# A decoder block's last stages: output tiles of the last two units from another pool and their LayerNorms in another order, m of y_a's second half in z's tiles, and later splits of y_a's weights, y_a's first input and T1

## The chip, the cores and the metric

The kernel runs on one NeuronCore of a Trainium2 chip. Its engines are TensorE (PE in the profile), VectorE (DVE), ScalarE (ACT), GpSimd (POOL) and SyncE (SP), which here only issues DMAs. Each engine works through its own instructions in the order in which they were issued; semaphores tie the engines together. The metric is the time of one execution in microseconds of device time, the median of several runs.

## The reference

The block takes x (2048 positions by 1024 channels, float32) and computes, cut to what matters:

```python
proj = x @ w_in + b_in                      # q, k, v, g_attn, u_lru, g_lru, gate_logits
attn = combine(dilated_attention(q, k, v))  # three head groups, weighted by softmax of their lse
y_a = (attn * silu(g_attn)) @ w_attn_proj
h = rg_lru(causal_conv(u_lru))
y_b = (h * silu(g_lru)) @ w_lru_proj
merged = sigmoid(gA) * y_a + sigmoid(gB) * y_b
out = merged @ w_out + b_out
x = layer_norm(alpha * x + out) * ln_gain + ln_bias
```

## The kernel before, in words

Each float32 product is made of three matmuls of a fast format: an operand is split into a high part h (ScalarE copies it) and a low part l (VectorE subtracts h), and h·h, h·l and l·h are added in PSUM. Such a split is one `split` of lines 1134 (ScalarE) and 1135 (VectorE), and it waits for the load of its operand. The engines' order is the order of the code (a manual schedule). Two lists move work: `later(lag, fn)` runs fn in the `run(late)` that comes lag steps on, `pe_later` does so in the middle of a step's matmuls.

Five stages follow each other on TensorE. The projection (line 636) takes 1400 us, attention 220. Then:

- **y_b**, 32 steps `yb_job(n)` of 24 matmuls, four chunks c of 512 positions by eight feature tiles f. A step first runs what is due (splits, stores), has SP load gB of step n + 2, makes its matmuls, and VectorE evacuates the tile into gB (line 1372, the evacuation), which SP stores a step later. Beside it branch A is combined: `combine` loads three head groups' outputs, `mix` has TensorE spread the weights into a bank bc (line 1315, three banks), VectorE multiplies (1316), GpSimd adds (1318, 1319), and SP stores to at_scr. In steps 23 to 31 y_a's weights wa, its input at (four parts for the first chunk) and w_out's blocks woB are loaded and, some steps later, split.
- **y_a**, 32 steps `ya_job(i)` of twelve matmuls, 2.72 us each. A tile needs its weight wa and all four input parts of its chunk; the low part of an input is read by the second of each three matmuls. VectorE forms gA = (gA + 1)·y_a (line 1481), GpSimd adds y_b (1482). The sum m stays in SBUF for chunks 0 and 1 (tiles me); for chunks 2 and 3, i = 16 to 31, it is made in place in gA's tile and stored to m_scr (1484). gA and ybr are loaded three steps ahead; gA's tiles come from five buffers of tag gt, ybr's from four of tag rc.
- **z**, the output projection in Strassen-like form: 256 positions are a unit pair q (0 to 7) with seven products each, in the table `order`; T1 to T4 are differences of w_out's blocks, loaded in y_a's last steps and behind them. `prep_m` splits the m operand two products ahead (tiles mh and ml, three buffers each), ScalarE seeds banks with the bias (line 1593), `z_outs` on VectorE forms the results, among them bank Z from bank A (line 1609), into which the third and fourth products go.
- **LayerNorm** of unit (q, i), i = 0 or 1, follows in steps behind its products: sum and mean, square, factor, norm, gain (VectorE, into an output tile), bias (GpSimd, 229), store (SP, 1680). Output tiles have tag rc, four buffers. The last pair q = 7 has a form of its own: `bn_stats` and an aggregate on VectorE (1699, 1703), the factor on GpSimd, `last_centre` (1709), and then for i = 0 a scale on ScalarE (1767) and the bias on GpSimd, for i = 1 both in one on VectorE (1714).

NZ is the number of products in `order`; the last product is NZ - 1.

Of the kernel before, what the change touches and what calls it, by code (L numbers as in the profile page):

```python
# [15 lines left out]
P = 128  # L16
# [15 lines left out]
def hybrid_block_kernel(ctx: ExitStack, tc: tile.TileContext, a: dict, out: bass.AP):  # L32
# [63 lines left out]
    def later(lag, fn):  # L96
        late.append((now["n"] + lag, fn))
# [1226 lines left out]
    def prep_wa(f, lag):  # L1324
        if f % 4 == 0:
            WA["t"] = big(("X3", "X4")[f // 4], [P, 4, 2, 4, P], F32R, f"wa{f}")
        t = WA[f] = WA["t"][:, f % 4]
        sp.dma_start(flat(t[:, 1]), wf_scr[f][:, 0:4])
        later(lag, lambda: split(t[:, 0], t[:, 1]))
# [86 lines left out]
    for n in range(32):  # L1416
        if n >= 1:
            next(blocks_of_out, None)
        c, f = divmod(n, 8)
        if c + 1 < NCH:  # L1420
            for k in range(2 * f, 2 * f + 2) if f < 4 else ():
                load_h(c + 1, k, min(k + 2, 7) - f)
        elif f < 4:
            for k in range(2 * f, 2 * f + 2):
                prep_wa(k, k + 2 - f if k < 6 else 4)
        for _ in range(2 if n in (23, 24, 28, 29, 30, 31) else 0):
            load_wo(*wo_raw.pop(0))
        if n == 26:
            for k in range(4):
                load_at(0, k, k + 2)  # L1430
        for k in range(1 if 26 <= n < 30 else 2 if n >= 30 else 0):
            later(0, lambda q=wo.pop(0): split_wo(*q))
        yb_job(n)
        if n >= 30:
            load_ya(n - 30)
        if n in cmb:
            combine(*cmb[n])
            if cmb[n][1] == 0:
                pe_later(1, lambda c=cmb[n][0]: spread(c))
        if n == 0:  # L1440
            load_stats()
        if n == 1:
            weigh()
    load_ya(2)
    for _ in range(5):
        run(late)
        run(pe_late)
        now["n"] += 1
# [16 lines left out]
    def ya_job(i):  # L1465
        c, f = divmod(i, 8)
        if i + 3 < 32:
            load_ya(i + 3)
        ga, yb = YG.pop(i)
        if i == 4:  # L1470
            ya = fp.tile([P, 4, P], F32, tag="ct", name=f"ya{c}{f}", bufs=1).rearrange("p b q -> p (b q)")
        else:
            ya = fp.tile([P, CH], F32, tag="y", name=f"ya{c}{f}", bufs=4)
        for k in range(4):
            xx = AT[c][:, k]
            pe.matmul(ya, WA[f][:, 0, k], xx[:, 0], start=(k == 0), stop=False)
            pe.matmul(ya, WA[f][:, 0, k], xx[:, 1], start=False, stop=False)
            pe.matmul(ya, WA[f][:, 1, k], xx[:, 0], start=False, stop=(k == 3))
        if f == 0 and c < 2:
            ME[c] = big(("Z0", "Z1")[c], [P, 8, CH], F32, f"me{c}")  # L1480
        dve.scalar_tensor_tensor(out=ga, in0=ga, scalar=1.0, in1=ya, op0=ALU.add, op1=ALU.mult)
        pool.tensor_tensor(out=ME[c][:, f] if c < 2 else ga, in0=ga, in1=yb, op=ALU.add)
        if c > 1:
            later(1, lambda: sp.dma_start(m_scr[c][:, f], ga))

    def load_x(q, i):
        tt_ = 2 * q + i
# [50 lines left out]
    for i in range(32):  # L1538
        run(late)
        c, f = divmod(i, 8)  # L1540
        if f == 0 and c + 1 < NCH:
            for k in range(4):
                load_at(c + 1, k, k + 4)
        if i in (2, 4, 6):
            load_vec(i // 2 - 1)
        if i == 10:
            dve.tensor_tensor(out=vec[0][:, CH:], in0=vec[0][:, CH:], in1=vec[0][:, 0:CH], op=ALU.subtract)
        if i in (8, 10, 12, 14):
            load_x(i // 4 - 2, i // 2 % 2)
        ya_job(i)  # L1550
        if wo:
            split_wo(*wo.pop(0))
        if 24 <= i < 28:
            load_tb("T1", i - 24)
        if i >= 28:
            load_tb("T2", i - 28)
            split_tb("T1", i - 28)
            if i < 30:
                prep_m(order[i - 28][0], UNIT[order[i - 28][1]])
        now["n"] += 1  # L1560
# [101 lines left out]
            act.activation(of(q, n), of(q, n), AF.Identity, scale=s[:, 10:11], bias=s[:, 11:12])  # L1662

    def out_tile(q, i, j):
        y = stats[q, i, j] = rc_p.tile([P, CH], F32, tag="rc", name=f"y{q}{i}{j}")
        return y

    def ln_gain(q, i):
# [38 lines left out]
    def last_centre(q, i, j):  # L1707
        mv = small(q, i)
        dve.scalar_tensor_tensor(out=out_tile(q, i, j), in0=of(q, LN[i][j]), scalar=mv[:, 0:1], in1=vec[1][:, SIDE[j]],
                                 op0=ALU.subtract, op1=ALU.mult)  # L1710

    def last_scale(q, i, j):
        y = stats[q, i, j]
        dve.scalar_tensor_tensor(out=y, in0=y, scalar=small(q, i)[:, 2:3], in1=vec[2][:, SIDE[j]], op0=ALU.mult, op1=ALU.add)

    whole, half_a, half_b = slice(0, CH), slice(0, CH // 2), slice(CH // 2, CH)
    for q in range(NQZ):
        for i in range(2):
            if q == NQZ - 1:
                continue  # L1720
            ready = [max(place[q, 6], place[q, 3]), place[q, 2]] if i == 0 else [place[q, 7], place[q, 4]]
            for j, (n, r) in enumerate(zip(LN[i][::-1], ready)):
                on(r + 1, "sum", ln_sum, q, i, j, n)
            g = max(ready) + 1
            for k, fn, d in (("mean", ln_mean, 1), ("square", ln_square, 2), ("factor", ln_factor, 3), ("norm", ln_norm, 4),
                             ("gain", ln_gain, 5), ("bias", ln_bias, 6), ("store", ln_store, 7)):
                d -= q + i == 0 and d > 1
                on(g + d, k, fn, q, i)
        for p, n in ((5, "C"), (1, "A")):
            if place[q, p] > 2:  # L1730
                on(*((place[2, 5] - 1, "seed late") if q == 2 else (max(place[q, p] - 3, 0), "seed")), seed, q, n)
        if q >= 2:
            on(place[q - 2, 6] + 1, "load", load_x, q, 0)
            on(place[q - 2, 7] + 1, "load", load_x, q, 1)
        for n, p in (("S1", 5), ("S2", 6), ("S3", 7), ("S4", 3)):
            on(max(place[q, p] - 4, 0), "add", add_m, q, n)
    for c in (2, 3):
        on(max(place[2 * c - 3, p] for p in (2, 3, 4)) - 1, "load", load_me, c)
    for n, g in (("T2", (0, 1, 2, 3)), ("T3", (3, 4, 5, 6)), ("T4", (7, 8, 9, 10))):
        for k in range(4):  # L1740
            on(g[k], "split", split_tb, n, k)
    for q in range(2):
        seed(q, "A")
# [9 lines left out]
        do(g, "store")  # L1753
    q = NQZ - 1
    z_product(NZ - 1)
    do(NZ - 1, "factor", "bias", "gain", "norm", "store")
    bn(q, 0, "C", whole, 1)
    last_mean(q, 0, 2)
    bn(q, 1, "Z1", half_a, 1)
    for j in range(2):  # L1760
        last_centre(q, 0, j)
    bn(q, 1, "Z1", half_b, 2)
    last_mean(q, 1, 3)
    do(NZ, "norm", "bias", "gain", "store")
    for j in range(2):
        last_centre(q, 1, j)
        act.activation(stats[q, 0, j], stats[q, 0, j], AF.Copy, scale=small(q, 0)[:, 2:3])
    ln_bias(q, 0)
    do(NZ + 1, "gain", "bias", "store")
    do(NZ + 2, "bias", "store")  # L1770
    do(NZ + 3, "store")
    for j in range(2):
        last_scale(q, 1, j)
        send(q, 0, j, sp)
# [61 lines left out]
```

## Time and profile before

| | us |
|---|---|
| three runs | 2083.02, 2086.12, 2087.07 |
| median | 2086.12 |
| the profiled execution | 2080.2 |
| its span | 2078.4 |
| TensorE busy | 2045.3 |
| VectorE busy | 1649.2 |
| ScalarE busy | 1185.8 |
| GpSimd busy | 589.3 |

The profile is of one execution. In its timeline a row has a start and a duration in us, the engine, the line of the code, the operation, out<-in, shapes and a count of merged instructions; in brackets stands how long the engine was idle before it and what released it. A letter q behind an engine's name is its queue (SPq issues DMAs). A row of the waits reads: who, waited for whom, us in total, times, longest. A row of windows gives busy time and counts of PE, PEld, DVE, ACT and POOL in a stretch, then the granted clock of TensorE as a share, and the DMA's share and rate. A row "x12" of the chain of waits merges twelve instructions. The kernel's stages lie at about 1624 to 1816 us (y_b), 1816 to 1903 (y_a), 1907 to 2063 (z) and 2063 to 2078 (the end).

### The profile page before, as it was taken

The numbers are of one execution on the slowest core, as the hardware profiler recorded it, in microseconds if no ns is written. First come the engines' busy times: TensorE is split into PE (matmuls) and PEld (weight loads), VectorE is DVE, ScalarE is ACT, GpSimd is POOL, SyncE is SP. The second block draws the span as 40 slices with busy tenths as digits, with TensorE's granted clock in tenths as the row PEclk, the third lists the DMA queues.
The fourth block names the chain that finished last, engine by engine and source line by source line (L and its number), as shares of the span: only waits on it lengthen the run. The fifth ranks groups of instructions, "written<-read, shape, count | busy, mean of one in ns | idle before, by whom it ended". The sixth has DMA issues, their size and how long they took to land.

```text
span 2078.4 us, 35466 instructions
## 1 busy us (share of the span) xinstructions
PE 2045.3 (98%) x11588; PEld 1686.9 (81%) x11588; DVE 1649.2 (79%) x3080; ACT 1185.8 (57%) x2482; POOL 589.3 (28%) x597
## 2 busy tenths in 40 slices
PE   8999999999999999999999999999999999999997
PEld 7888888888888888888887888888888888787885
DVE  8888789788889778778878888877999655545776
ACT  6447356446356565667666657567999411212674
POOL 1111111111111013222222232221425234355686
PEclk9999999999999999999999999999999999999998
DMA  8987989988988977778788879789896899998441
GB/s 271 275 250 247 267 271 249 284 249 271 252 280 245 324 242 196 224 212 247 231 259 264 282 223 260 246 230 357 331 340 197 256 321 314 320 375 269 142 153 71
DMA packets 379736, 535.16 MB, mean 257 GB/s; under 512 B 174816, under 2 KB 179936, under 8 KB 376032
## 3 DMA queue, kind: packets, MB, share of 16 engines
q1 hardware_dynamic: 363552, 507.12, 75.8%
q0 software_dynamic: 12256, 19.42, 5.6%
q10 hardware_dynamic: 3744, 6.36, 0.9%
q8 instruction: 92, 1.51, 0.3%
q14 instruction: 92, 0.75, 0.1%
HBM read 323.43 MB, written 193.59 MB: 249 GB/s over the span
## 4 chain that ended last, share of the span: by engine, by line
PE 75%; DMA 12%; ACT 5%; DVE 4%; SPq 2%; issue 1%; POOL 0%; DVEq 0%; POOLq 0%; ACTq 0%
PE q L636 57%; ACT p L1055 4%; PE A L1601 3%; PE o L1096 2%; PE C L1601 2%; PE Z L1601 2%; PE s L1040 2%; PE yb L1366 1%; PE yb L1367 1%; DMA at_scr<-oc 1%; PE yb L1368 1%; PE pt L1066 1%; PE g L497 1%; DMA m_scr<-gA 1%; SPq L309 1%
## 5 line engine op out<-in xcount | busy, mean ns | idle before, releaser
L636 PE MATMUL q<-xT,hS 128*128 128x512 f32 x1680 | 519.3, 390 | 0.0
L636 PE MATMUL q<-xT,l 128*128 128x512 f32 x1120 | 436.1, 389 | 0.0
L636 PE MATMUL q<-xB,hA 128*128 128x512 f32 x1248 | 388.2, 392 | 5.6 <-ACT xB L217 5.6
L636 PEld LDWEIGHTS q<-xT,hS 128*128 128x128 f32 x1680 | 314.4, 188 | 69.6 <-issue 5.2
L636 PE MATMUL q<-xB,l 128*128 128x512 f32 x904 | 353.0, 390 | 0.0
L636 PEld LDWEIGHTS q<-xB,hA 128*128 128x128 f32 x1248 | 235.0, 189 | 57.6 <-ACT xB L217 5.6
L636 PEld LDWEIGHTS q<-xT,l 128*128 128x128 f32 x1120 | 210.3, 188 | 43.8
L636 PEld LDWEIGHTS q<-xB,l 128*128 128x128 f32 x904 | 170.5, 189 | 35.6
L247 POOL DMA_DIRECT2D wS<-in_w_in_dram x70 | 61.8, 964 | 478.3 <-DMA wS<-in_w_in_dram 145.1
L1055 ACT ACTIVATE p<-p,sta 128x256 f32<-128x256 f32 (+1 forms) x384 | 172.9, 473 | 1.1 <-DVE sta L1047 1.1
L636 PE MATMUL q<-xT,hA 128*128 128x512 f32 x560 | 173.1, 391 | 0.0
L636 PE MATMUL q<-xB,hS 128*128 128x512 f32 x560 | 173.0, 390 | 0.0
L271 ACT ACTIVATE hA<-wA 128x512 fp32r<-128x512 f32 x218 | 134.0, 623 | 48.1 <-DMA wA<-in_w_in_dram 11.8
L271 ACT ACTIVATE hS<-S 128x512 fp32r<-128x512 f32 x175 | 107.9, 623 | 84.2 <-DVE S L229 17.9
L229 POOL TENSOR_TENSOR S<-S,wA 128x512 f32<-128x512 f32 x35 | 49.8, 1424 | 356.2 <-DVE S L229 210.2
L636 PEld LDWEIGHTS q<-xT,hA 128*128 128x128 f32 x560 | 104.8, 188 | 23.3 <-issue 1.8
L636 PEld LDWEIGHTS q<-xB,hS 128*128 128x128 f32 x560 | 104.8, 188 | 23.0 <-issue 1.5
L1047 DVE CUSTOM_DVE_ANT_0 p<-s,mask 128x256 f32<-128x256 f32 (+1 forms) x384 | 118.0, 376 | 0.2 <-PE s L1040 0.2
L1366 PE MATMUL yb<-h,wl 128*128 128x512 f32 x256 | 100.4, 392 | 0.0
L1367 PE MATMUL yb<-h,wl 128*128 128x512 f32 x256 | 99.9, 390 | 0.0
L1368 PE MATMUL yb<-h,wl 128*128 128x512 f32 x256 | 99.8, 390 | 0.0
L229 DVE TENSOR_TENSOR l<-wA,hA 128x512 fp32r<-128x512 f32 x113 | 78.0, 693 | 27.2 <-ACT hA L271 24.6
(455 smaller groups left out, 4289.3 us busy)
## 6 DMA issues: line engine op xcount, KB each, us to landing
wA<-in_w_in_dram SPq DMA_DIRECT2D x253, 256.0 KB, 4.6
wl_scr<-l SPq DMA_DIRECT2D x105, 512.0 KB, 4.9
l<-wl_scr SPq DMA_DIRECT2D x105, 512.0 KB, 4.5
sw<-y SPq DMA_DIRECT2D x384, 64.0 KB, 3.2
wS<-in_w_in_dram SPq DMA_DIRECT2D x70, 256.0 KB, 4.5
wS<-in_w_in_dram POOLq DMA_DIRECT2D x70, 256.0 KB, 6.6
v_scr<-vs SPq DMA_DIRECT2D x192, 64.0 KB, 3.7
B<-k_scr SPq DMA_DIRECT2D x24, 512.0 KB, 7.0
```

Of the source, the lines that this page charges most:

```text
L229: eng.tensor_tensor(out=out, in0=in0, in1=in1, op=op)
L247: pool.dma_start(t, w_part(s, x), accum_op=ALU.add)
L271: act.activation(h, r, AF.Copy)
L636: pe.matmul(bank, w[:, ks], x[:, kk, xx], start=(first and i == 0 and not onto), stop=(last and i == 11), skip_group_check=onto)
L1040: pe.matmul(s[h][:, j, lo:256], A[hs, x, n * P:(n + 1) * P], k, start=(x + y == 0), stop=(y == 1 or g == 2))
L1047: dve.tensor_tensor_reduce(out=st["p", i, j][:, h, lo:256], in0=st["s", i, j // 2][h][:, j % 2, lo:256], in1=mask[:, lo:256], scale=1.0, s ...
L1055: act.activation(p, p, AF.Exp, scale=-1.0, bias=s[:, h:h + 1], accum_out=s[:, 2 + h:3 + h])
L1096: pe.matmul(o[hs, j, :], V[:, n if x else prev(g, n), v0:v0 + 64], ptb[:, j % 2, x, h, :], start=(x == first(i, j) // P), stop=(x == 1))
L1366: pe.matmul(yb, WL[f][:, 0, k], xx[:, 0], start=(k == 0), stop=False)
L1367: pe.matmul(yb, WL[f][:, 0, k], xx[:, 1], start=False, stop=False)
L1368: pe.matmul(yb, WL[f][:, 1, k], xx[:, 0], start=False, stop=(k == 7))
L1601: pe.matmul(b[:, cs], x[:, k], w[:, k, y, cs], start=False, stop=(k == 3 and n == 2), skip_group_check=True)
```

## The change

- **Output tiles.** The four output tiles of q = 7 get tag gt (five buffers), the rest keep rc.
- **LayerNorm of unit (6, 1)**: square and factor stand one product earlier, norm, gain, bias and store two. In the code after the last product the order is written anew: (7, 0) is centred, scaled on ScalarE and biased on GpSimd before the second unit's statistics, half by half between its steps.
- **m of y_a's second half**: for i = 16 to 27 m goes to a tile of tag mh or ml (z's, three buffers each) instead of gA's tile, and is stored from there.
- **Splits**: of the weights wa 2 to 4 steps later (lag k + 4 - f), of at's first chunk two steps later (k + 4); the loop behind y_b's steps has one round more. T1's four splits stood in y_a's steps 28 to 31; now two stand in steps 30 and 31, and two behind z's products 0 and 1, T2 to T4 moving back by one to three products. No load is issued elsewhere.

The diff, cut to its core:

```diff
-                prep_wa(k, k + 2 - f if k < 6 else 4)
+                prep_wa(k, k + 4 - f)
...
-                load_at(0, k, k + 2)
+                load_at(0, k, k + 4)
...
-    for _ in range(5):
+    for _ in range(6):
         run(late)
...
-        pool.tensor_tensor(out=ME[c][:, f] if c < 2 else ga, in0=ga, in1=yb, op=ALU.add)
+        m = ME[c][:, f] if c < 2 else ga if i >= 28 else vx_p.tile([P, CH], F32, tag=("mh", "ml")[i % 2], name=f"m{i}", bufs=3)
+        pool.tensor_tensor(out=m, in0=ga, in1=yb, op=ALU.add)
         if c > 1:
-            later(1, lambda: sp.dma_start(m_scr[c][:, f], ga))
+            later(1, lambda: sp.dma_start(m_scr[c][:, f], m))
...
-            split_tb("T1", i - 28)
+            if i >= 30:
+                split_tb("T1", i - 30)
...
-        y = stats[q, i, j] = rc_p.tile([P, CH], F32, tag="rc", name=f"y{q}{i}{j}")
+        y = stats[q, i, j] = rc_p.tile([P, CH], F32, tag="rc" if q < NQZ - 1 else "gt", name=f"y{q}{i}{j}", bufs=4 if q < NQZ - 1 else 5)
...
+    def last_bias(j):
+        y = stats[NQZ - 1, 0, j]
+        tt(pool, y, y, vec[2][:, SIDE[j]], ALU.add)
...
-                d -= q + i == 0 and d > 1
+                d -= (q + i == 0 and d > 1) + (q == NQZ - 2 and i == 1) * ((d > 1) + (d > 3))
...
-    for n, g in (("T2", (0, 1, 2, 3)), ("T3", (3, 4, 5, 6)), ("T4", (7, 8, 9, 10))):
+    for n, g in (("T1", (0, 0, 0, 1)), ("T2", (2, 3, 4, 5)), ("T3", (5, 6, 7, 8)), ("T4", (8, 9, 10, 10))):
...
     z_product(NZ - 1)
-    do(NZ - 1, "factor", "bias", "gain", "norm", "store")
+    do(NZ - 1, "bias", "gain", "store")
     bn(q, 0, "C", whole, 1)
     last_mean(q, 0, 2)
-    bn(q, 1, "Z1", half_a, 1)
+    do(NZ, "bias", "store")
     for j in range(2):
         last_centre(q, 0, j)
+        act.activation(stats[q, 0, j], stats[q, 0, j], AF.Copy, scale=small(q, 0)[:, 2:3])
+    last_bias(0)
+    bn(q, 1, "Z1", half_a, 1)
     bn(q, 1, "Z1", half_b, 2)
     last_mean(q, 1, 3)
-    do(NZ, "norm", "bias", "gain", "store")
+    last_bias(1)
     for j in range(2):
         last_centre(q, 1, j)
-        act.activation(stats[q, 0, j], stats[q, 0, j], AF.Copy, scale=small(q, 0)[:, 2:3])
-    ln_bias(q, 0)
-    do(NZ + 1, "gain", "bias", "store")
-    do(NZ + 2, "bias", "store")
-    do(NZ + 3, "store")
```

VectorE at the end of y_b, before the change, from behind the evacuation of step 29 (gB tiles 20277 and 20327 are those of steps 30 and 31, at the input's parts, wa weights):

```order
L1135 TENSOR_TENSOR wa_20172<-wa_20172 128x512
L1135 TENSOR_TENSOR at_20175<-at_20175 128x512
L1135 TENSOR_TENSOR woB_20267<-woB_20267 128x512 x2
L1372 SCALAR_TENSOR_TENSOR gB_20277<-gB_20277,yb_20380 128x512
L1135 TENSOR_TENSOR wa_20172<-wa_20172 128x512
L1135 TENSOR_TENSOR at_20175<-at_20175 128x512
L1135 TENSOR_TENSOR wa_20172<-wa_20172 128x512 x2
L1135 TENSOR_TENSOR woB_20267<-woB_20267 128x512 x2
L1372 SCALAR_TENSOR_TENSOR gB_20327<-gB_20327,yb_20425 128x512
```

The two at rows are the third and fourth part of the input; the first two stand earlier, before the evacuations of steps 28 and 29. The same place with the change (gB tiles 20271 and 20319 are those of steps 30 and 31):

```order
L1135 TENSOR_TENSOR wa_20082<-wa_20082 128x512
L1135 TENSOR_TENSOR at_20175<-at_20175 128x512
L1135 TENSOR_TENSOR woB_20263<-woB_20263 128x512 x2
L1372 SCALAR_TENSOR_TENSOR gB_20271<-gB_20271,yb_20372 128x512
L1135 TENSOR_TENSOR wa_20082<-wa_20082 128x512
L1135 TENSOR_TENSOR at_20175<-at_20175 128x512
L1135 TENSOR_TENSOR woB_20263<-woB_20263 128x512 x2
L1372 SCALAR_TENSOR_TENSOR gB_20319<-gB_20319,yb_20413 128x512
L1135 TENSOR_TENSOR wa_20172<-wa_20172 128x512
L1135 TENSOR_TENSOR at_20175<-at_20175 128x512
L1135 TENSOR_TENSOR wa_20172<-wa_20172 128x512
L1135 TENSOR_TENSOR at_20175<-at_20175 128x512
```

Now all four input parts are split behind evacuation 29: the first before that of step 30, the second before that of step 31, the third and fourth behind it.

ScalarE between y_a and z, before (toT_21014 is T1, A the banks that the first two products add to, L1593 their seeds):

```order
L1134 ACTIVATE toT_21014<-toT_21014 128x512
L1523 ACTIVATE mh0A_21103<-me_20489 128x512
L1134 ACTIVATE toT_21014<-toT_21014 128x512
L1523 ACTIVATE mh1A_21126<-me_20489 128x512
L1134 ACTIVATE toT_21014<-toT_21014 128x512 x2
L1593 ACTIVATE A_21194<-vec_20515 128x512
L1593 ACTIVATE A_21196<-vec_20515 128x512
```

And with the change (T1 is toT_21023, the seeds are at L1595):

```order
L1524 ACTIVATE mh0A_21113<-me_20489 128x512
L1524 ACTIVATE mh1A_21134<-me_20489 128x512
L1134 ACTIVATE toT_21023<-toT_21023 128x512 x2
L1595 ACTIVATE A_21202<-vec_20515 128x512
L1595 ACTIVATE A_21204<-vec_20515 128x512
L1524 ACTIVATE mh0A_21218<-me_20489 128x512
L1134 ACTIVATE toT_21023<-toT_21023 128x512
```

Two of T1's splits stand ahead of the seeds where there were four, and the operands of the first two products stand ahead of all of them.

VectorE at the very end, with the change, from the results of the last product but two (y_22587 and y_22589 are the gains of unit (6, 1), y_22645 and y_22647 the tiles of unit (7, 1)):

```order
L229 TENSOR_TENSOR A_22388<-x_22265,A_22388 128x512
L229 TENSOR_TENSOR y_22587<-Z_22424,vec_20561 128x512
L229 TENSOR_TENSOR y_22589<-A_22235,vec_20561 128x512
L1701 BN_STATS st_22591<-Z_22476 128x6
L1701 BN_STATS st_22593<-A_22388 128x6
L229 TENSOR_TENSOR C_22363<-x_22208,C_22363 128x512
L1701 BN_STATS st_22591<-C_22363 128x6
L1705 BN_AGGR mv_22625<-st_22591 128x2
L1711 SCALAR_TENSOR_TENSOR y_22631<-Z_22476,mv_22625,vec_20561 128x512
L1711 SCALAR_TENSOR_TENSOR y_22634<-C_22363,mv_22625,vec_20561 128x512
L1701 BN_STATS st_22593<-Z_22572 128x6 x2
L1705 BN_AGGR mv_22640<-st_22593 128x2
```

Before, the two gains stood behind the second aggregate, directly ahead of the tiles of (7, 1).

More of the change, by code (lines that the diff above doesn't have):

```diff
@@ L1738, in hybrid_block_kernel @@
         on(max(place[2 * c - 3, p] for p in (2, 3, 4)) - 1, "load", load_me, c)
-    for n, g in (("T2", (0, 1, 2, 3)), ("T3", (3, 4, 5, 6)), ("T4", (7, 8, 9, 10))):
-        for k in range(4):
+    for n, g in (("T1", (0, 0, 0, 1)), ("T2", (2, 3, 4, 5)), ("T3", (5, 6, 7, 8)), ("T4", (8, 9, 10, 10))):
+        for k in range(2 if n == "T1" else 0, 4):
             on(g[k], "split", split_tb, n, k)
```

## The prediction

> **What bounds the kernel now.** I read the page first, then TensorE's waits, then the timeline at the places that the waits name.
>
> ```profile
> span 2078.4 us, 35466 instructions
> PE 2045.3 (98%) x11588; PEld 1686.9 (81%) x11588; DVE 1649.2 (79%) x3080; ACT 1185.8 (57%) x2482; POOL 589.3 (28%) x597
> PE A L1601 <- ACT A L1593: 3.1, 1, 3.1
> PE bc L1315 <- DVE oc L1316: 2.6, 1, 2.6
> PE Z L1601 <- DVE Z L1609: 1.2, 2, 0.9
> ```
>
> TensorE is busy 98% of the span, so no edit that leaves its matmuls alone can gain more than its idle time: about 33 us. The three waits above are the large ones late in the program, and all lie where the diff works. The rest worth having is the tail, after the last matmul:
>
> ```profile
> 2062.76 0.28 PE L1601 MATMUL Z<-toT,ml7A 128*128 128x256 f32 x1
> 2061.68 0.21 DVE L1703 BATCH_NORM_AGGREGATE mv<-st 128x2 f32<-128x12 f32 x1
> 2062.23 0.55 POOL L229 TENSOR_TENSOR mv<-mv,konst 128x1 f32<-128x1 f32 x1
> 2064.25 1.33 ACT L1767 ACTIVATE y<-y,mv 128x512 f32<-128x512 f32 x2 [4.36 <-issue]
> 2065.35 0.63 DVE L229 TENSOR_TENSOR y<-Z,vec 128x512 f32<-128x512 f32 x1
> 2066.30 4.92 POOL L229 TENSOR_TENSOR y<-y,vec 128x512 f32<-128x512 f32 x4
> 2072.11 0.75 DVE L1709 SCALAR_TENSOR_TENSOR y<-Z,mv,vec 128x512 f32<-128x512 f32 x1 [5.54 <-DMA out_dram<-y]
> 2074.04 1.41 DVE L1714 SCALAR_TENSOR_TENSOR y<-y,mv,vec 128x512 f32<-128x512 f32 x2
> ```
>
> TensorE ends at 2063.04 and the span 15.4 us later. In it VectorE stands 5.54 us until an older output store has landed: the last unit's tile reuses a buffer of the unit before it, whose biases are among the four on GpSimd (1.23 each).
>
> **Part 1: the tail.** Two edits meet. The last four output tiles leave the four-buffer pool, so the 5.54 us wait has nothing left to wait for. And the LayerNorm of unit (6,1) moves up: its two gains stand before the statistics of (7,0) on VectorE, its biases run on GpSimd before the last products' results are due. What is late next is a chain through four engines, priced from the rows above. The two gains push the aggregate from 2061.68 by at most 2 x 0.60 = 1.2, to 2062.9 (the 0.23 idle before it absorbs a little). Its factor is ready 1.10 after the aggregate starts (2061.68 to 2062.78 before), at 2064.0. ScalarE scales one tile in 0.66: 2064.7. GpSimd adds its bias in 1.23: 2065.9. Behind that bias now stands the factor of (7,1), 0.9 more: 2066.8. VectorE's two last scalings take 1.41: 2068.3. From their end to the span's end it was 2078.4 - 2075.45 = 2.95 before; so 2071.2, a gain of 7.2. Three stores leave within a microsecond instead of two, so I take **-7.0**. Ends: -7.5 if the 0.23 idle counts and nothing queues; -5.5 if the four biases that now stand ahead of the factor hold GpSimd 1.5 us too long (an estimate: each 0.4 over its 1.23).
>
> **Part 2: y_a into z.** Here TensorE waits 3.07 us, and then runs at half clock:
>
> ```profile
> SPq L1382 <- DMA m_scr<-gA: 18.2, 11, 2.5
> 1903.19 0.39 PE L1478 MATMUL ya<-at,wa 128*128 128x512 f32 x1
> 1905.48 0.63 ACT L1134 ACTIVATE toT<-toT 128x512 fp32r<-128x512 f32 x1 [2.17 <-DMA toT<-wt_scrT]
> 1906.65 1.22 PE L1601 MATMUL A<-woB,mh0A 128*128 128x512 f32 x2 [3.07 <-ACT A L1593]
> 1908.00:1909.00 1.00, 1.00 (x4) 0.71 (x4) 0.00 (x0) 0.00 (x0) 0.00 (x0) 0.50 1.01 318
> 1910.88 0.62 PE L1601 MATMUL A<-woB,mh1A 128*128 128x512 f32 x2
> 1948.65 2.72 PE C L1601 x12
> 1909.17 0.69 DVE L1481 SCALAR_TENSOR_TENSOR gA<-gA,ya 128x512 f32<-128x512 f32 x1 [3.75 <-DMA gA<-mg_scr]
> 1912.09 1.78 DVE L1135 TENSOR_TENSOR toT<-toT 128x512 fp32r<-128x512 f32 x1
> 1913.80 0.68 DVE L1609 SCALAR_TENSOR_TENSOR Z<-x,A 128x512 f32<-128x512 f32 x1
> 1917.19 0.68 DVE L1609 SCALAR_TENSOR_TENSOR Z<-x,A 128x512 f32<-128x512 f32 x1
> 1920.86 0.62 PE L1601 MATMUL C<-toT,mh0S 128*128 128x512 f32 x2
> ```
>
> The chain runs back from the seed of bank A on ScalarE, through the split of T1's fourth part ahead of it, to that part's load, to SP, which stood 18.2 us in all on stores of m: gA's tile could not be loaded again before its m had left. With m in a tile of its own (through step 27) SP waits for GpSimd alone, one step behind TensorE; so gA's last load and T1's lie ready. T1's third and fourth splits also move behind the seeds. Then the first product follows the last y_a matmul at once: 3.07 gone, and 4.23 - 2.72 = 1.51 of slow matmuls (1906.65 to 1910.88 for twelve). VectorE still has to make Z twice; the sequence from line 1481's last row is the same in kind (split, ml, split, Z, ml, split, Z), so Z ends 5.31 and 8.70 after it starts. It would start at 1903.6, when TensorE is done, not 1909.17. TensorE could start the third product at 1903.42 + 5.44 = 1908.86 and gets it at 1909.1 (0.15 behind Z as before); the fourth at 1912.45 rather than 1911.8; the fifth at 1915.2. It was 1920.86: **-5.7**. Ends: -6.6 with no Z wait at all, -2.1 if two further splits that now fall into the products (fourteen instead of twelve, up to 1.78 each) come back as waits.
>
> Free here: GpSimd writes m elsewhere at the same size. A tile is used again six steps (16 us) later; were a store that late, GpSimd would wait for it. T2 to T4's splits stand two or more products ahead of their use.
>
> **Part 3: y_b into y_a.** This is the part that I think goes wrong.
>
> ```profile
> 1798.24 0.39 PE L1368 MATMUL yb<-h,wl 128*128 128x512 f32 x1
> 1798.59 0.63 ACT L1134 ACTIVATE at<-at 128x512 fp32r<-128x512 f32 x1 [6.33 <-DMA at<-at_scr]
> 1800.46 1.88 DVE L1316 TENSOR_TENSOR oc<-oc,bc 128x512 f32<-128x512 f32 x3
> 1801.20 1.69 PE L1315 MATMUL bc<-wT,sel 128*128 128x512 f32 x3 [2.57 <-DVE oc L1316]
> 1802.73 0.40 PE L1366 MATMUL yb<-h,wl 128*128 128x512 f32 x1
> ```
>
> ScalarE and VectorE stood in line at the split of y_a's input, whose load had not landed, and the mix of branch A behind it held TensorE's bc banks. With lags of 4 the split waits for nothing, and TensorE passes: 1802.73 - 1798.47 - 0.69 = 3.57 us earlier from there. But the splits now stand behind the last y_b evacuations (line 1372), each of which needs its gB:
>
> ```profile
> SPq L1309 <- DMA at_scr<-oc: 8.9, 3, 3.8
> 1812.52 0.45 SPq L1355 DMA_DIRECT2D gB<-mg_scr  x1
> DMA to landing us min/median/max: 5.4/5.5/5.6
> 1811.90 0.69 DVE L1372 SCALAR_TENSOR_TENSOR gB<-gB,yb 128x512 f32<-128x512 f32 x1 [2.78 <-DMA gB<-mg_scr]
> 1815.06 0.69 DVE L1372 SCALAR_TENSOR_TENSOR gB<-gB,yb 128x512 f32<-128x512 f32 x1
> 1815.66 0.69 DVE L1135 TENSOR_TENSOR wa<-wa 128x512 fp32r<-128x512 f32 x1
> 1816.26 0.69 DVE L1135 TENSOR_TENSOR at<-at 128x512 fp32r<-128x512 f32 x1
> 1816.38 0.39 PE L1476 MATMUL ya<-at,wa 128*128 128x512 f32 x1
> 1819.27 0.68 DVE L1372 SCALAR_TENSOR_TENSOR gB<-gB,yb 128x512 f32<-128x512 f32 x1
> ```
>
> SP's largest wait here (1775 to 1825 us) is for landings of its own stores; the diff moves none of its y_b issues, so the gB loads land when they did: the last at 1812.52 + 5.5 = 1818.0. VectorE was already 3 us behind (1819.27, with TensorE done at 1816.4), which cost nothing, since y_a's four input splits were ahead of it. Now evacuation 29 (1811.90) precedes the first input split, 30 (1815.06) the second, 31 the third and fourth. TensorE comes to y_a at 1816.38 - 3.57 = 1812.8 and meets these waits one by one. VectorE: evacuation 31 at 1818.07, then, 0.60 apart, a weight, input 3, a weight, input 4, done at 1820.47 + 0.69 = 1821.16. Of y_a's first tile two matmuls remain; the second tile starts at 1821.7. It started at 1816.38 + 2.72 = 1819.1: **+2.6**; the 3.57 is not cashed, it is waited off and more. Queued behind VectorE there is only GpSimd's first m, which has y_a's other banks as cover. Ends: -3.6 if nothing waits, +4.1 if the clock also falls.
>
> That is the open price. The trace has both: the clock fell to 0.50 behind a gap of 3.07, and stayed at 1.00 across 1798.6 to 1802.7, where only three matmuls ran and the longest gap was 2.57. The new gaps come out as 0.7, 2.3, 2.1 and 0.4 us (inputs 1 to 4 done at 1813.8, 1816.95, 1819.96 and 1821.16, with three matmuls, 0.9, between); they are nearest to the row that kept the clock, so I take no loss. [...]
>
> **Sum.** -7.0 - 5.7 + 2.6 = -10.1 us. The profiled execution took 2080.2 (span 2078.4 and 1.8 around it) and would take 2070.1. The median of the three runs stands 5.9 above it; taken off that median, 2086.1 - 10.1 = **2076.0**.
>
> **The rivals.**
> - *Half clock at y_a's start.* For it: little work in 8.4 us, and 3.07 sufficed elsewhere; against: the 1.00 above. Some 1.5 us lost as after 1906.65: 2077.5.
> - *No wait at y_a's start.* Loads land earlier, because less is queued. Against: SP's order and its waits there are its own. The 3.57 is cashed: 2076.0 - 2.6 - 3.6 = 2069.8.
> - *Splits come back in z.* VectorE has no gap from 1909 to 1926 already; two more splits at 1.78 are 3.6: 2079.6. For it: VectorE's splits take 1.78 beside a busy GpSimd. Against: the later products have slack, and the list of waits has none behind the fifth product.
> - *Slower: the wait at y_a's start grows.* In-order VectorE behind three gB loads, each microsecond that the last lands later is a microsecond of TensorE. It cancels the gain from 10.1 on (landing at 1828) and is slower by over 0.2% from 14.3 on, 2090.3 and more. For it: the place is real; against: the last gB landed 5.5 us after its issue, and nothing new stands in SP's queue ahead of it.
>
> That an edit does nothing can be ruled out for the tail and for the T1 splits: the order of the instructions shows both.
>
> **How the numbers follow.** Forecast 0.42, half clock 0.30, no wait 0.08, splits return (or part of the tail's gain is lost) 0.15, the long wait 0.05. The range runs from 2070.5 (forecast with -7.5 and -6.6, and run spread: the three before differ by 4) to 2082 (half clock with the splits' return, or the tail at -5.5); it leaves out the no-wait case and the long wait. About 0.2%, 4.2 us, is what a measurement of this kernel can tell from no change. Faster by more: the first three cases and half of the fourth, 0.88; within: 0.08; slower: 0.04.
>
> **What would show it.** Right: no wait of VectorE on an output store after the last matmul, and some 8 us from that matmul to the end; no gap and full clock between y_a and z, two short Z waits; no bc wait late in y_b; four waits of TensorE on line 1135's splits in y_a's first tile, the last ended about 4 us after the last gB landed. Wrong: y_a's first tile in one run of 2.7 us; the clock at 0.5 behind it; waits of TensorE on toT splits or Z after the fifth product; a tail above 10 us.

## The result, and the profile after

Six runs of the changed kernel lie between 2076.4 and 2079.6 us with a median of 2078.4; six of the kernel before beside them between 2083.0 and 2087.8 with a median of 2086.0. The ratio is 0.9964, 95% interval 0.9951 to 0.9976: 7.6 us faster. The prediction was 2076.0 in a range of 2070.5 to 2082.

The profiled execution after took 2079.4 us, only 0.8 under the one before, because that one stood 5.9 us under its own median. So I don't compare the two ends. I compare stages, counted from one mark: the third group of bc matmuls from the end of y_b (1780.70 before, 1785.51 after). Nothing that the diff moves runs ahead of it. The mark before and after:

```profile
1780.70 0.86 PE L1315 MATMUL bc<-wT,sel 128*128 128x512 f32 x3
1785.51 0.86 PE L1315 MATMUL bc<-wT,sel 128*128 128x512 f32 x3
```

| stage, us | before | after | difference | predicted |
|---|---|---|---|---|
| mark to y_a's first matmul | 35.68 | 32.08 | -3.60 | -3.57 |
| y_a's first to last matmul | 86.81 | 96.72 | +9.91 | +6.2 |
| to z's fifth product | 17.67 | 12.14 | -5.53 | -5.7 |
| to the last matmul's end | 142.18 | 142.13 | 0 | 0 |
| to the span's end | 15.36 | 9.02 | -6.3 | -7.0 |
| sum | 297.70 | 292.09 | -5.6 | -10.1 |

The page after, its first line and that of the engines:

```profile
span 2077.6 us, 35458 instructions
PE 2049.9 (99%) x11588; PEld 1687.4 (81%) x11588; DVE 1639.7 (79%) x3080; ACT 1186.9 (57%) x2482; POOL 590.1 (28%) x597
```

TensorE is busier with the same 11588 matmuls: 2049.9 for 2045.3. Busy time grew here with a slower clock (its mean was 0.994 for 0.996, and at 0.50 a y_a matmul takes 0.63 us for 0.39), so the 33 us of idle time that the prediction takes as the most to be gained are no strict bound. The list of its waits after, the rows that stand where the three large ones stood:

```profile
PE ya L1477 <- DVE at L1135: 5.1, 3, 2.3
PE Z L1603 <- DVE Z L1611: 0.4, 1, 0.4
PE ya L1476 <- ACT at L1134: 0.3, 1, 0.3
```

The waits on bc and on the seed of A are gone; a new one of 5.1 us stands at y_a's start. TensorE and VectorE there, in the timeline after:

```profile
1817.59 0.39 PE L1476 MATMUL ya<-at,wa 128*128 128x512 f32 x1
1818.34 0.69 DVE L1372 SCALAR_TENSOR_TENSOR gB<-gB,yb 128x512 f32<-128x512 f32 x1 [4.87 <-DMA gB<-mg_scr]
1820.29 0.50 PE L1477 MATMUL ya<-at,wa 128*128 128x512 f32 x1 [2.31 <-DVE at L1135]
1823.38 0.79 PE L1477 MATMUL ya<-at,wa 128*128 128x512 f32 x1 [1.36 <-DVE at L1135]
1824.62 0.69 DVE L1372 SCALAR_TENSOR_TENSOR gB<-gB,yb 128x512 f32<-128x512 f32 x1
1826.57 0.79 PE L1477 MATMUL ya<-at,wa 128*128 128x512 f32 x1 [1.47 <-DVE at L1135]
1827.04 0.69 DVE L1135 TENSOR_TENSOR at<-at 128x512 fp32r<-128x512 f32 x1
1828.87 0.63 PE L1476 MATMUL ya<-at,wa 128*128 128x512 f32 x1
1831.76 0.39 PE L1477 MATMUL ya<-at,wa 128*128 128x512 f32 x1
```

Evacuation 29 waits for its gB until 1818.34, evacuation 31 stands at 1824.62, and the last split of the input behind it ends at 1827.7. The first tile takes 11.28 us (1817.59 to 1828.87), where it took 2.72. The durations tell the rest: a matmul of 0.39 becomes 0.63 to 0.79. A window of one microsecond there has, in the third column from the right, the granted clock:

```profile
1822.00:1823.00 1.00, 0.02 (x1) 0.00 (x0) 1.00 (x3) 1.00 (x2) 0.00 (x0) 0.50 1.04 399
```

The half clock lasts until 1831.8, three microseconds into full work. The start of z after, and SP's waits there:

```profile
1914.31 0.39 PE L1478 MATMUL ya<-at,wa 128*128 128x512 f32 x1
1914.54 0.62 PE L1603 MATMUL A<-woB,mh0A 128*128 128x512 f32 x2
1923.64 0.70 PE L1603 MATMUL Z<-woB,mh1A 128*128 128x512 f32 x2 [0.40 <-DVE Z L1611]
1926.45 0.62 PE L1603 MATMUL C<-toT,mh0S 128*128 128x512 f32 x2
```
```profile
SPq L1485 <- POOL m L1483: 13.8, 12, 1.7
```

The first product follows the last y_a matmul within a matmul's pitch, and SP waits for GpSimd instead of for the landing of m's stores. The end after:

```profile
2068.08 0.21 DVE L1705 BATCH_NORM_AGGREGATE mv<-st 128x2 f32<-128x12 f32 x1
2068.30 0.28 PE L1603 MATMUL Z<-toT,ml7A 128*128 128x256 f32 x1
2070.71 0.75 DVE L1711 SCALAR_TENSOR_TENSOR y<-Z,mv,vec 128x512 f32<-128x512 f32 x1
2072.03 1.26 POOL L229 TENSOR_TENSOR y<-y,vec 128x512 f32<-128x512 f32 x1
2072.10 2.40 DVE L1720 SCALAR_TENSOR_TENSOR y<-y,mv,vec 128x512 f32<-128x512 f32 x2
```

The 5.54 us on an output store are gone. What is new is the last row: two scalings take 2.40 us where they took 1.41, while GpSimd adds a bias.

### The profile page after: what moved, and what is told of

Read it like the earlier page. It is cut to its first block, busy times and chain, and to the rows that moved or that the text cites. A ratio compares the mean times of both kernels' runs of the same rounds, so it can differ in the third digit from the quotient of the medians.

```text
span 2077.6 us, 35458 instructions
## 1 busy us (share of the span) xinstructions
PE 2049.9 (99%) x11588; PEld 1687.4 (81%) x11588; DVE 1639.7 (79%) x3080; ACT 1186.9 (57%) x2482; POOL 590.1 (28%) x597
## 4 chain that ended last, share of the span: by engine, by line
PE 85%; ACT 7%; DMA 5%; DVE 1%; SPq 1%; issue 1%; POOL 0%; DVEq 0%; POOLq 0%; ACTq 0%
PE q L636 63%; ACT p L1055 6%; PE A L1603 3%; PE yb L1366 2%; PE yb L1367 2%; PE yb L1368 2%; PE C L1603 2%; PE Z L1603 2%; PE ya L1477 1%; PE ya L1478 1%; PE ya L1476 1%; PE g L497 1%; PE o L1096 1%; DMA at_scr<-oc 1%; ACT ptb L1079 1%; PE pt L1066 1%
## 5 line engine op out<-in xcount | busy, mean ns | idle before, releaser
L271 ACT ACTIVATE hS<-S 128x512 fp32r<-128x512 f32 x175 | 107.8, 623 | 83.7 <-DVE S L229 16.1
```

The source lines that it names most:

```text
L271: act.activation(h, r, AF.Copy)
```

## The experiments

My theory after the result: the three edits act at three places and add up, and the third loses all that the two profiles differ by at y_b's end and y_a's start. Each part was run alone, the third also undone. Then the disputed place was taken apart. The stages of every profile, counted from the same mark, stand in a table behind the first five experiments. Gains in us are worked out from the ratio, where the medians are not named; the difference of two medians can be up to 1.5 us off that.

**The end alone.** The kernel before with the output tiles in the other pool and the last LayerNorms in the new order:

```diff
-        y = stats[q, i, j] = rc_p.tile([P, CH], F32, tag="rc", name=f"y{q}{i}{j}")
+        y = stats[q, i, j] = rc_p.tile([P, CH], F32, tag="rc" if q < NQZ - 1 else "gt", name=f"y{q}{i}{j}", bufs=4 if q < NQZ - 1 else 5)
...
-                d -= q + i == 0 and d > 1
+                d -= (q + i == 0 and d > 1) + (q == NQZ - 2 and i == 1) * ((d > 1) + (d > 3))
...
```

> The kernel before with the first edit alone (output tiles of the last pair in other buffers, the last LayerNorms reordered). Theory (the three parts act at three places and add up): 6.3 us under the kernel before, as the two traces' ends differ; from the last matmul's end to the span's end 9.0 us instead of 15.4, no wait of VectorE on an output store, the rest of the timeline as before. Rival (the end is bound by the stores and the last unit's own chain): 2 us or less, with the idle time in front of the last scalings instead.

Median 2079.2 beside 2085.4; ratio 0.9970 (0.9959 to 0.9980), 6.3 us less. From the last matmul to the end 9.07 us. The theory holds and the rival falls. The run changes both the pool of the output tiles and the order of the LayerNorms, so it doesn't tell what each would give alone.

**The second edit alone.** The kernel before with m in z's tiles and T1's splits moved:

```diff
+        m = ME[c][:, f] if c < 2 else ga if i >= 28 else vx_p.tile([P, CH], F32, tag=("mh", "ml")[i % 2], name=f"m{i}", bufs=3)
...
-            split_tb("T1", i - 28)
+            if i >= 30:
+                split_tb("T1", i - 30)
...
+    for n, g in (("T1", (0, 0, 0, 1)), ("T2", (2, 3, 4, 5)), ("T3", (5, 6, 7, 8)), ("T4", (8, 9, 10, 10))):
...
```

Read from this table, T2's and T3's splits move back by two products and T4's by one or none, and not by one to three as the section on the change has it.

> The kernel before with the second edit alone (m of the second half in z's tiles, T1's splits later). Theory: 5.5 us under the kernel before; last y_a matmul to fifth product 12.1 us instead of 17.7, the wait of 3.1 us on the seed of A gone, two waits on Z of 0.3 to 0.9 us left. Rival (the gain came with the later splits of y_a's weights, which change what is queued): 0 to 2 us, the seed still late.

Median 2079.2; ratio 0.9973 (0.9959 to 0.9988), 5.6 us less; 12.18 us from the last y_a matmul to the fifth product, no wait on the seed. It holds, without the third edit.

**The third edit alone.**

```diff
-                prep_wa(k, k + 2 - f if k < 6 else 4)
+                prep_wa(k, k + 4 - f)
...
-                load_at(0, k, k + 2)
+                load_at(0, k, k + 4)
...
-    for _ in range(5):
+    for _ in range(6):
```

> The kernel before with the third edit alone (y_a's weights and first input split later). Theory: it loses what the traces differ by over y_b and y_a together, 6.3 us above the kernel before: the bc wait of 2.6 us is gone, y_a's first tile takes 11 us instead of 2.7 and runs partly at half clock. Rival (the first tile is late for another reason, such as m's stores from other tiles or z's splits): the bc wait is gone and nothing is lost, 3.6 us under the kernel before.

Median 2087.6; ratio 1.0005 (0.9996 to 1.0014): between 0.8 us less and 2.9 more. Both theories miss. The mechanism is there, in TensorE's waits:

```profile
PE ya L1477 <- DVE at L1135: 4.8, 3, 1.8
PE ya L1476 <- ACT at L1134: 0.3, 1, 0.3
```

y_a takes 95.46 us instead of 86.81; but that is not a loss of 6 us against the kernel before.

**The third edit undone in the changed kernel** (the same lines the other way round):

> The changed kernel with the third edit undone. Theory: 6.3 us under the changed kernel (12 us under the kernel before): the bc wait of 2.6 us is back, y_a's first tile takes 2.7 us at full clock, the end and the start of z stay as in the changed kernel. Rival (m's stores or the reordering need the later splits): the bc wait is back and nothing is won, 3.6 us above the changed kernel.

Median 2077.2; ratio to before 0.9957 (0.9944 to 0.9971), nominally 1 to 3 us better than the changed kernel (0.9964, and 0.9971 on another chip) and not separable from it. The theory's 6.3 falls here too, and this profile shows why. ScalarE and TensorE late in y_b:

```profile
1804.83 0.63 ACT L1134 ACTIVATE at<-at 128x512 fp32r<-128x512 f32 x1 [7.31 <-DMA at<-at_scr]
1807.44 1.99 PE L1315 MATMUL bc<-wT,sel 128*128 128x512 f32 x3 [5.69 <-DVE oc L1316]
```

The bc wait is not 2.57 us but 5.69, because the load of y_a's input landed later. The clock then fell (from 1809.23 to 1812.2 a matmul takes 0.63 us for 0.39), so that 41.21 us passed from the mark to y_a's first matmul.

This run also tests whether the first two edits add up. Its stages show both gains in full (9.1 us at the end, 12.17 us to the fifth product). By the ratios it gains 9.0 us (6.0 to 11.7), where the two alone sum to 11.9; the intervals don't separate these.

**The two kernels as they are, once more**, for a second profile of each:

> The kernel before as it is, for a second profile. Theory (its first profile caught a mild case): the bc wait is 2.5 to 5.7 us with the clock at half behind it, and from the seventh-to-last step of y_b to y_a's first matmul it takes 37 to 41 us instead of 35.7. Rival (the first profile is typical, and the variants changed it): the wait is again 2.6 us at full clock, 35.7 us.

> The changed kernel as it is, beside the others on one chip and for a second profile. Theory (the times of y_b's end and y_a's start hang on when the loads of y_a's input and of gB land, which differs from one execution to the next): about 2078.4 us, 1.3 us or so above the kernel with the third edit undone; y_a's first tile again 10 to 12 us. Rival (the third edit costs the 6 us by which the two first profiles differ there): 5 us or more above it.

The changed kernel: 2078.8 beside 2084.0, ratio 0.9971 (0.9960 to 0.9982), and stage for stage the same as its first profile. The kernel before once more, its wait and a window behind it:

```profile
1805.70 1.69 PE L1315 MATMUL bc<-wT,sel 128*128 128x512 f32 x3 [2.67 <-DVE oc L1316]
```
```profile
1808.00:1810.00 2.00, 2.00 (x6) 1.54 (x5) 2.00 (x3) 0.00 (x0) 1.92 (x2) 0.50 0.97 336
```

A gap of 2.67 us, about that of the first profile, but here with half clock behind it: 37.35 us for the stage. So the theory holds: the first profile caught the mildest case of seven, by the time of the stage.

| profile | bc wait | mark to y_a | y_a | to fifth product | end |
|---|---|---|---|---|---|
| before | 2.57 | 35.68 | 86.81 | 17.67 | 15.4 |
| before, again | 2.67 | 37.35 | 86.82 | 16.18 | 15.5 |
| the end alone | 4.56 | 40.16 | 86.82 | 18.20 | 9.1 |
| second edit alone | 2.54 | 37.23 | 86.81 | 12.18 | 15.4 |
| m alone | 4.19 | 39.75 | 86.82 | 12.17 | 15.5 |
| T1 alone | 4.44 | 39.49 | 86.82 | 19.94 | 15.4 |
| third edit undone | 5.69 | 41.21 | 86.82 | 12.17 | 9.1 |
| changed | 0 | 32.08 | 96.72 | 12.14 | 9.0 |
| changed, again | 0 | 32.08 | 96.64 | 12.17 | 9.1 |
| third edit alone | 0 | 32.08 | 95.46 | 16.14 | 15.4 |
| filled waits | 0 | 32.08 | 95.56 | 12.18 | 9.0 |
| splits in step 29 | 0 | 32.08 | 88.18 | 12.14 | 9.0 |
| the same, VectorE's bias | 0 | 32.08 | 88.98 | 12.18 | 8.5 |
| the same, weights early | 0 | 32.39 | 90.39 | 12.18 | 9.0 |

With the old places of the splits (first seven rows) the first stage takes 38.70 us on average, 6.6 over the 32.08 of the new ones. With the new places y_a takes 96.27 on average (changed twice, third edit alone), 9.45 over 86.82. The third edit costs the difference, 2.8 us by these means; the first two profiles showed 6.3. The first profile of before was 3.0 us better here than the mean of its kind, half of the 5.9 by which it stood under its median.

**m alone**, with T1's splits at their old places (the first line of the second diff):

> The kernel before with m of the second half in z's tiles alone, T1's splits where they were. Theory (SP was held by the landing of m's stores, which held gA's and T1's loads): nearly all of the second edit, 5.0 to 5.6 us under the kernel before; the fifth product 12 to 13 us behind the last y_a matmul. Rival (the seeds come late because four splits stand ahead of them): 1.5 us or less, and TensorE still waits 2 us or more for a seed.

Median 2081.6 beside 2086.1; ratio 0.9975 (0.9965 to 0.9984), 5.2 us less, 12.17 us to the fifth product: all of the second edit. SP's largest wait there:

```profile
SPq L1485 <- POOL m L1483: 11.3, 11, 1.7
```

**T1's splits alone**, with m in gA's tile (the other lines of it):

> The kernel before with T1's splits moved (two in steps 30 and 31, two behind products 0 and 1) alone, m where it was. Theory (the last gA and T1 still land late behind m's stores): within 1.5 us of the kernel before, the fifth product 16 us or more behind the last y_a matmul, the wait on the seed replaced by one on Z. Rival (the order ahead of the seeds is the cause): 4 to 5.5 us under it, 12 to 13 us.

Median 2086.9; ratio 1.0003 (0.9993 to 1.0013), no gain. The waits of SP, of TensorE, and VectorE's row that ends TensorE's:

```profile
SPq L1382 <- DMA m_scr<-gA: 20.2, 11, 2.5
```
```profile
PE Z L1602 <- ACT toT L1134: 6.1, 1, 6.1
```
```profile
1918.76 0.69 DVE L1481 SCALAR_TENSOR_TENSOR gA<-gA,ya 128x512 f32<-128x512 f32 x1 [2.28 <-DMA m_scr<-gA]
1923.31 0.68 DVE L1610 SCALAR_TENSOR_TENSOR Z<-x,A 128x512 f32<-128x512 f32 x1
```

The seeds come early, and TensorE passes the first products without a gap; then it stands 6.1 us at the third. The list names a split on ScalarE, but the end of the gap (1924.14) is that of Z on VectorE. VectorE's last evacuation of y_a waits for a gA tile whose m had not left, and Z stands behind it. The theory holds: the stores of m were the cause, and the order ahead of the seeds only chose where TensorE would meet them.

**The waits at y_a's start filled with matmuls.** The changed kernel with 28 matmuls that nobody reads:

```diff
...
+            for _ in range(8 * (k < 3) + 4 * (k == 3) if i == 0 else 0):
+                pe.matmul(fill, WA[0][:, 0, 0], AT[0][:, 0, 0], start=True, stop=True)
             pe.matmul(ya, WA[f][:, 0, k], xx[:, 1], start=False, stop=False)
```

> The changed kernel with 28 added matmuls into an unused bank inside y_a's first tile, eight ahead of the second matmul of each of the first three inputs and four ahead of that of the fourth (they compute nothing that is used). Theory (the clock falls because TensorE stands between the split inputs, and this is a cost of its own): the clock stays at 1.00, the waits end when they did, and 1.4 to 2.7 us under the changed kernel. Rival (the waits on the splits are the whole loss, the clock nothing): within 0.5 us of the changed kernel.

Median 2074.8 beside 2078.8 for the changed kernel on the same chip; ratios to before 0.9959 (0.9946 to 0.9973) and 0.9971, so that the intervals overlap. In the profile y_a takes 1.1 us less than in the changed kernel; but it took 95.46 with the third edit alone, without any added matmul, so this difference by itself shows nothing. A window in the place, and TensorE's and VectorE's rows of the first tile's end:

```profile
1817.00:1818.00 1.00, 0.70 (x4) 0.53 (x4) 1.00 (x2) 0.76 (x2) 0.00 (x0) 1.00 0.88 283
```
```profile
1820.71 0.69 DVE L1372 SCALAR_TENSOR_TENSOR gB<-gB,yb 128x512 f32<-128x512 f32 x1 [0.21 <-DMA gB<-mg_scr]
1823.12 0.69 DVE L1135 TENSOR_TENSOR at<-at 128x512 fp32r<-128x512 f32 x1
1824.85 0.39 PE L1478 MATMUL ya<-at,wa 128*128 128x512 f32 x1
```

The clock stays at 1.00, and everything behind the first tile runs at full speed: 84.09 us from the second tile's start (1824.85) to the last y_a matmul, as in the kernel before, where the changed kernel took 85.44. The tile itself is no shorter (11.47 for 11.28): it still ends on the splits, and its added matmuls take time of their own. So the clock is a cost of its own, 1.35 us behind the tile, and the waits are the larger part. The size of that cost differs: 1.36 us in the changed kernel's second profile, 0.71 with the third edit alone, whose clock came back sooner. That is the theory's mechanism, a little under its range in the profile; the 4 us between the medians can't be told from it.

**All four input splits in step 29**, one to four steps earlier than in the changed kernel and ahead of the last three evacuations:

```diff
-                load_at(0, k, k + 4)
+                load_at(0, k, 3)
```

> The changed kernel with the four splits of y_a's first input set in step 29 of y_b, behind the load's landing and ahead of the last three evacuations. Theory (the place of the four splits in VectorE's row is all that the third edit loses): no bc wait, no wait of TensorE in y_a's first tile, which takes 2.7 us at full clock: 9.9 us under the changed kernel's profile, some 15 us under the kernel before. Rival (the wait only moves: the first tiles also need the banks that the last evacuations free): TensorE waits for line 1372 at y_a's second to fourth tile instead, and 3 us or less are won.

Median 2073.9 beside 2078.8 for the changed kernel and 2084.0 for the one before; ratio 0.9948 (0.9936 to 0.9961). VectorE's and TensorE's rows:

```profile
1806.15 2.49 DVE L1135 TENSOR_TENSOR at<-at 128x512 fp32r<-128x512 f32 x4
1814.70 0.69 DVE L1372 SCALAR_TENSOR_TENSOR gB<-gB,yb 128x512 f32<-128x512 f32 x1 [3.66 <-DMA gB<-mg_scr]
1816.28 0.39 PE L1476 MATMUL ya<-at,wa 128*128 128x512 f32 x1
1819.00 0.39 PE L1476 MATMUL ya<-at,wa 128*128 128x512 f32 x1
1833.86 0.69 DVE L1481 SCALAR_TENSOR_TENSOR gA<-gA,ya 128x512 f32<-128x512 f32 x1 [3.27 <-DMA gA<-mg_scr]
1835.06 1.78 DVE L1135 TENSOR_TENSOR at<-at 128x512 fp32r<-128x512 f32 x1
1841.50 0.50 PE L1477 MATMUL ya<-at,wa 128*128 128x512 f32 x1 [0.73 <-DVE at L1135]
```

ScalarE's copy of the first part still waits for the load's landing, until 1800.87; VectorE comes to the four splits later, at 1806.15, and does not wait. No bc wait, none on line 1372 as the rival had it, and the first tile in 2.72 us at full clock: the stages sum to 8.6 us less than the changed kernel's, for 9.9 expected. The rest lies at a new wait of 0.73 us, some 22 us behind the first tile, and at the matmuls slowed around it (y_a takes 88.18 us for 86.82): the second chunk's input splits stand behind an evacuation that waited 3.27 us for its gA. It is the same knot at the next place, and small. The medians show 5 us and not 8.6; the profiled execution was the shortest of five (2069.5; the others 2072.6 to 2075.4), so the other executions took longer at places that this profile can't show.

**The same with the weights' splits at their old places:**

```diff
-                prep_wa(k, k + 4 - f)
+                prep_wa(k, k + 2 - f if k < 6 else 4)
...
-    for _ in range(6):
+    for _ in range(5):
```

> The changed kernel with y_a's input splits in step 29 and its weights' splits back at their old places. Theory (the input's splits alone make the bc wait and the wait at y_a's start): no bc wait and no wait in y_a's first tile, within 1.5 us of the kernel that has the weights later too (2073.9 us). Rival (the weights' early splits hold VectorE, and with it the mix and TensorE's banks): a bc wait of 1 us or more comes back, 3 to 6 us above it.

Median 2073.1 beside 2086.1; ratio 0.9932 (0.9919 to 0.9946). TensorE's waits there:

```profile
PE ya L1477 <- DVE at L1135: 2.4, 4, 0.7
```

All four of them lie at the second chunk (1835.9 to 1840.5); no bc wait, none in the first tile. The theory holds in its waits, and by the medians (2073.1 for 2073.9). By the ratios this kernel is 3.3 us the faster, on another chip and with intervals that overlap. So of the third edit the input's four splits did both the good and the harm, and what the weights' places do is less than these runs can tell.

**The same with VectorE adding the last bias:**

```diff
     for j in range(2):
         last_centre(q, 0, j)
-        act.activation(stats[q, 0, j], stats[q, 0, j], AF.Copy, scale=small(q, 0)[:, 2:3])
+        if j == 0:
+            act.activation(stats[q, 0, j], stats[q, 0, j], AF.Copy, scale=small(q, 0)[:, 2:3])
...
-    last_bias(1)
     for j in range(2):
         last_centre(q, 1, j)
+    last_scale(q, 0, 1)
```

> The kernel with y_a's input splits in step 29, and beside that the last bias of unit (7, 0) no longer on GpSimd beside VectorE's last scalings: its tile is scaled and biased in one instruction on VectorE, as a third. Theory (the two last scalings took 2.40 instead of 1.41 us because GpSimd adds a bias at the same time): three in about 2.0 us, the end 8.5 to 8.7 us instead of 9.0; and a second profile of y_a's start: no wait in its first tile, waits of up to some 4 us at later loads, since the five runs of the kernel without this edit lay between 2069.5 and 2075.4 us. Rival (VectorE's own work bounds the end): a third scaling costs 0.7, the end 9.7 us.

Median 2069.8 beside 2086.1; ratio 0.9915 (0.9901 to 0.9929): the best of these kernels, 17.7 us under the one before by the ratio, 16.3 by the medians. The last scalings, and TensorE's waits at y_a:

```profile
2062.05 2.07 DVE L1720 SCALAR_TENSOR_TENSOR y<-y,mv,vec 128x512 f32<-128x512 f32 x3
```
```profile
PE ya L1477 <- DVE at L1135: 1.5, 2, 0.7
```

Three scalings in 2.07 us where two took 2.40, and an end of 8.50. The edit is worth 0.5; that the ratio is 3.3 thousandths (7 us) better than without it is not its doing, and what it is stays open: the two ran on different chips, four and five times, and their stages differ by 0.3 us.

## Why the prediction was right, and where it was not

The direction, the place that "goes wrong" and the two gains were right. The total was 2.4 us too good, by the medians.

- **The end: -7.0 predicted, -6.3 measured.** The chain came as worked out: aggregate 0.86 later against the last matmul (at most 1.2 predicted), last scalings from 3.52 us behind TensorE's end (3.8 predicted). The term that was mis-sized is the two scalings: they were priced from a row without GpSimd beside them, at 1.41; in the new order GpSimd's second bias runs with them, and they took 2.40. The kernel with that bias on VectorE took 0.5 of it back.
- **y_a into z: -5.7 predicted, -5.53 measured.** The wait on the seed went, the clock stayed up, the Z waits are 0.4 and less. One reason was incomplete: the T1 splits' move was named as part of the cure, and m's tiles alone give all of it. T1's move alone turns the wait on the seed into one of 6.1 us on Z. The size hangs on the execution too: without the edit the stage took 16.1 to 18.2 us in four profiles (before, before again, the end alone, the third edit alone), 4.9 us on average over the 12.16 with it.
- **y_b: -3.57 predicted, -3.60 in the first pair of profiles.** That agreement is luck of the sample. In seven profiles with the old places the stage took 3.6 to 9.1 us more than with the new ones, 6.6 on average, since the wait hangs on a load's landing (the input's first split stands 17.8 to 21.6 us behind the mark) and the clock falls within it or behind it in six of the seven (matmuls of 0.63 us for 0.39 behind the gaps of 2.67, 4.19 and 5.69). Most of that spread comes from SP, which issued the load 12.3 to 15.0 us behind the mark; each part then landed 5.2 to 6.7 us after its issue.
- **y_a's first tile: +6.2 predicted, +9.9 measured.** The waits on line 1135's splits came where they were forecast, but three of the four (2.31, 1.36 and 1.47 us, with 0.3 on ScalarE's copy beside them): the fourth input's split was done before TensorE, by then slow, came to it. The step that failed is "the gB loads land when they did": counted from the mark, evacuation 29 came 1.6 us later than before (32.8 for 31.2 us) and evacuation 31 1.7 later than planned. SP issued the load of evacuation 29 0.9 us later behind the mark, and it took 7.3 us to land instead of 6.5; why, with the order of SP's issues unmoved, the runs don't show. But 31.2 was the earliest of the seven profiles with the old places (31.2 to 35.4), and in the seven without a bc wait this evacuation stands at 30.5 to 33.1 us: the prediction took one execution's time as fixed. The other half is the rival "half clock", which had a chance of 0.30: 1.35 us in the full work behind the tile, and some 0.6 within (1.14 us from the last split's end to the second tile, where 0.54 were planned). Taking the row that had kept the clock at 1.00 as the nearest was the wrong choice; the filled kernel shows the price.
- **Net of the third edit: +2.6 predicted; +6.3 in the first pair of profiles, 2.8 by the means over the profiles.** Both halves were too small, by 3.0 and 3.3 us, and nearly cancel, so that the net came out right by luck. The runs agree with the means: alone it costs between -0.8 and +2.9 us, undone it gains nothing separable.
- **The sum: -10.1 predicted, -7.6 measured.** By the means of the table the stages give -6.3 - 4.9 + 2.8 = -8.4 us, inside the interval of the measured ratio (5.0 to 10.2 us); the first pair of profiles, at -5.6, was a poor sample of the difference.

SP's rows of the load of evacuation 29, before (24.6 us behind the mark) and after (25.5):

```profile
1805.30 0.48 SPq L1355 DMA_DIRECT2D gB<-mg_scr  x1
1810.98 0.45 SPq L1355 DMA_DIRECT2D gB<-mg_scr  x1
```

The rival "slower" did not come, since the last gB landed under 2 us late and not 10 (39.0 us behind the mark for 37.4). "Splits come back in z" did not come either: the one wait left there is 0.4 us on Z. Its remark that VectorE has no gap from 1909 to 1926 was a misreading; in the trace before VectorE stands from 1910.5 to 1912.1.

## What to carry to other kernels

The wait for a DMA's landing had no fixed price here: in seven profiles of one place it was 2.5 to 5.7 us, and with the clock 3.6 to 9.1, so take such a term from several executions before you weigh it against another. In the row of an engine that works in order, as VectorE did when it stood 4.87 us at evacuation 29 with y_a's splits behind it, put work that TensorE needs next behind its own load but ahead of any instruction that waits for another: four splits moved by one to four steps were worth 5 us by the medians, and the bc wait that their first move was to cure stayed away. When a stage is moved, reprice its instructions by what will run beside them: the two last scalings took 1.41 us with GpSimd idle and 2.40 beside its bias.

## What the hardware showed that was not expected

The granted clock fell at gaps that differ little from ones that kept it: at y_b's end 2.57 us kept 1.00, 2.54 and 2.67 were followed by half clock for 3 to 4 us of full work. At y_a's start in the changed kernel it fell some 1.1 us behind the end of a gap of 2.31 us (1.00 up to 1821.2, 0.50 from 1821.4). So the length of a single gap did not decide it here; what did, the runs don't show.

Beside a GpSimd bias of 1.26 us, the first of the last two scalings took 1.74 us and the second, behind it, 0.74; in the kernel before, with GpSimd idle, they took 0.75 and 0.74. GpSimd started first (2072.03, VectorE 2072.10), and the scaling ended at 2073.84, 0.55 us behind the bias. With that bias on VectorE three scalings took 2.07 us. This is one pair of instructions; why the scaling took longer, the runs don't show.
